# Token-tile projections 512 columns wide, one run of attention, and covered tiles that are cleared later, in a two-layer hybrid decoder on one core

## The chip, the cores and the metric

The kernel runs on one core of a Trainium2 chip. The core has a matrix engine (TensorE: PE in the profile, with its weight loads as a row of their own, PEld), a vector engine (VectorE: DVE), a scalar engine (ScalarE: ACT), GpSimd (POOL) and a queue engine that issues most transfers (SyncE: SP). Matmuls write PSUM, which this program uses as eight buffers of 128 partitions by 512 float32 values, called banks here. The metric is the device time of one execution in microseconds. The kernel before takes 1861.66 us, the median of three runs (1861.14 to 1863.24).

## The reference

Two layers work on 512 tokens of width 1024. Each layer is a half-step SwiGLU, a mixer with three head groups on one projection, and another half-step SwiGLU:

```python
for l in range(DEPTH):                                   # DEPTH = 2
    x = x + 0.5 * swiglu(rms_norm(x, ffn1_norm[l]), ffn1_w_in[l], ffn1_w_out[l])
    h = rms_norm(x, mix_norm[l]) @ w_mix_in[l]
    (c_x, c_b, c_c, h_q, h_f, h_i, h_g, f_q, f_k, f_v, f_f) = split(h)
    y = concatenate([short_conv_mixer(c_x, c_b, c_c, ...),        # 256 channels
                     hgrn2_mixer(h_q, h_f, h_i, h_g, ...),        # 4 heads of 64
                     fox_mixer(f_q, f_k, f_v, f_f, ...)], -1)     # 8 heads of 64
    x = x + y @ w_mix_out[l]
    x = x + 0.5 * swiglu(rms_norm(x, ffn2_norm[l]), ffn2_w_in[l], ffn2_w_out[l])
```

`fox_mixer` is causal softmax attention. It normalises each head's queries and keys by their root mean square and adds a cumulated decay to the logits. Its queries, keys and values are 512 columns of `w_mix_in` each, 8 heads of 64. `hgrn2_mixer` is a gated linear recurrence in chunks of 64 tokens.

## The kernel before, in words

**Precision.** Each float32 operand is held as a high and a low part of a rounded type, and each product is three matmuls: high by high (line 308), high by low (314), low by high (315). The parts of a weight come from a cast on ScalarE (297 or 766) and a subtraction on VectorE (298 or 768). The tiles of parts are called `hl`, the loaded weights `st` or `w`.

**A stream.** `stream_steps` multiplies a strip of weights by the activations, two blocks of 128 rows at a time. Such a pair of blocks is a granule: one load into `st` (two buffers), one split into `hl` (three buffers), then its matmuls. It yields after each granule. In the last granule the jobs (one per output) are done one after another; in the others all jobs take the first block, and then all the second.

**The mixer.** Three projections come first. Then two generators `hgrn`, for two pairs of HGRN heads, run in turn. After each of their steps the host loop advances another generator, `projections`, by one granule, so that dense matmuls stand between the small ones of the recurrence. `projections` calls `fox_qkv` twice, for heads 0 to 3 and 4 to 7. Each call makes queries, keys and values with `tokens`: the stationary operand is a block of 128 tokens, 256 weight columns move, and four token tiles share two banks. That is 24 granules of 24 matmuls in a layer.

After a stream `fox_qkv` normalises. For queries and keys ScalarE squares a bank into the tile `qk` (1395), VectorE sums the squares (1396), six small instructions on 128x8 values follow, and VectorE multiplies the bank by the result into `qk` (1403). That multiplication is the last reader of the bank. For values ScalarE writes the high part (1409) and VectorE the low (1410).

Then `fox_attend` runs over 16 items (4 heads, 4 query tiles), twice. An item has scores (1450 to 1452), a softmax, transposes (1513) and, every second item, products with the values (1472). `fox_prep` (transposes at 1424) makes a head ready. Beside the first half stand the 12 granules of `conv` and beside the second the 12 of `most`, which is the output projection for six of the eight row blocks. From the third item on each item gets one granule.

**The banks.** `mm` has 3, `sc` 2, `pt` 2 and `po` 1. `tokens` takes `mm`, once also `po`. The outputs of `hgrn` go to `po`.

**The feed-forward part.** `plan` writes out a fixed order of products over three chunks of the hidden width. A product is 24 matmuls of 256 columns; a unit of two feed-forward tiles has seven (P1, P2, P6, P5, P7, P3, P4). P1, P6, P7 and P4 accumulate in one bank, P5 and P3 in another, and between P6 and P7 ScalarE has to copy the first bank (872); P5's bank is copied at 875, ahead of P3. At product n the weights of product n + 3 are split (766, 768), and `run(n)` starts loads and sums for later products. The orders on ScalarE and VectorE are fixed by `follow`.

The last three of the four feed-forward parts begin with four covered tiles (0 to 3) that are multiplied in the plain way while the operands of the plan are made ready (`enter`). `clear` scales two banks of such a tile by the norm (530, 531) and applies the gate (262, tile `gi`); `values` makes the hidden value (669, 666). The dictionary `entry` says after which product of the plan that is done. Tile 2 is cleared at product 5 and tile 3 at product 8.

Of the kernel before, what the change touches and what calls it, by code (L numbers as in the profile page):

```python
# [8 lines left out]
F32 = mybir.dt.float32  # L9
F32R = mybir.dt.float32r  # L10
# [3 lines left out]
AF = mybir.ActivationFunctionType  # L14
# [142 lines left out]
class Trunk:  # L157
# [383 lines left out]
    def enter(self, fp, w_in, then):  # L541
# [73 lines left out]
        def values(f, i):  # L615
# [106 lines left out]
    def halved(self, fp, w_in, w_out, covered):  # L722
# [116 lines left out]
        for n, (kind, w, p) in enumerate(seq):  # L839
# [128 lines left out]
    def mix(self, l, w, w_out, conv_w, out_gain, q_gain, k_gain, f_bias, next_gain):  # L968
# [3 lines left out]
        with tc.tile_pool(name=self.n("mix"), bufs=1) as mp:  # L972
# [38 lines left out]
            def tokens(a, banks=("mm", "mm")):  # L1011
                bs = [self.bank(t) for t in banks]
                jobs = []
                for i in range(4):
                    acc = bs[i // 2][:, 256 * (i % 2) : 256 * (i % 2) + 256]
                    jobs.append((acc, slice(0, 256), TOK[i]) + ((False,) if i % 2 else ()))
                yield from self.stream_steps(jobs, cols((a, 256)), self.xact, KD)
                return bs

            with tc.tile_pool(name=self.n("hg"), bufs=1) as hp:  # L1020
# [52 lines left out]
                half = [{}, {}]  # L1073

                def projections():
                    for hf in range(2):
                        yield from self.fox_qkv(mp, hf, tokens, half)

                dense = projections()
# [11 lines left out]
            with tc.tile_pool(name=self.n("at"), bufs=1) as ap_:  # L1091
# [16 lines left out]
                def beside(attend, dense):  # L1108
                    for n, _ in enumerate(attend):
                        if n >= 2:  # L1110
                            next(dense, None)
                    for _ in dense:
                        pass

                self.begin_norm(next_gain)
                order = [2, 3, 4, 5, 0, 1, 6, 7]
# [22 lines left out]
                beside(self.fox_attend(ap_, 0, half[0], qkg), conv())  # L1139
                beside(self.fox_attend(ap_, 1, half[1], qkg), most())  # L1140
# [42 lines left out]
    def hgrn(self, l, pr, hp, z, q, q2, v, sg, og):  # L1183
# [142 lines left out]
        ob = self.bank("po")  # L1326
# [59 lines left out]
    def fox_qkv(self, mp, hf, tokens, half):  # L1386
        nc = self.nc
        qk = mp.tile([P, 4, 4, 2, HD], F32, tag="qk", name=self.n("qk"), bufs=2)
        for w, a in enumerate((F_Q, F_K)):
            for bi, bank in enumerate((yield from tokens(a + 256 * hf, ("mm", "po" if w and not hf else "mm")))):  # L1390
                src = bank.rearrange("p (i h d) -> p i h d", i=2, h=4)
                s8 = lambda tag: mp.tile([P, 2, 4], F32, tag=tag, name=self.n(tag), bufs=2)
                out = qk[:, 2 * bi : 2 * bi + 2, :, w, :]
                m, r, t = s8("fm"), s8("fr"), s8("ft")
                nc.scalar.activation(out, src, AF.Square)
                nc.vector.reduce_sum(m, out, axis=AX.X)
                bc = lambda c: c[:, 2 * bi : 2 * bi + 2].unsqueeze(2).to_broadcast([P, 2, 4])
                nc.vector.tensor_mul(m, m, bc(self.inv2))
                self.act(r, m, AF.Ln, bias=self.epsc)
                self.act(r, r, AF.Exp, scale=-0.5)  # L1400
                self.rsqrt(r, m, r, t)
                nc.vector.tensor_mul(r, r, bc(self.invc))
# [217 lines left out]
```

## Time and profile before

| what | value |
|---|---|
| median of 3 runs | 1861.66 us |
| profiled execution, its own time | 1859.03 us |
| its span, first to last instruction | 1857.3 us |
| granted TensorE clock | 1.000 |
| layer 0: recurrence with the attention projections beside it | 391.31 to 484.10 us |
| layer 1: the same | 1307.83 to 1400.60 us |
| PE busy in the first of these | 91.41 of 92.79 us |

The busy time of PE is from rows whose ends are modelled: matmuls are pipelined, and a row of 0.28 us is followed 0.12 us later by the next. How long a matmul holds the engine is read from the starts of successive rows; a longer distance than usual between two starts is a wait, even where no idle time is shown. In rows of instructions the columns are start, length, engine, source line, operation, output and inputs, shape and count, and in brackets the idle time before and what ended it. In grouped rows they are busy time and mean length in ns, then idle time and what ended it. Several engines write two starts closer than the length of a row, for the same reason.

### The profile page before, as it was taken

How to read it: one execution, taken by the hardware profiler on the slowest of the kernel's cores; microseconds unless marked ns; L12 is line 12 of the kernel's file. 1: busy time of each engine (PE TensorE's matmuls, PEld its weight loads, DVE VectorE, ACT ScalarE, POOL GpSimd, SP SyncE). 2: the span in 40 equal slices, each digit the busy share in tenths (PEclk: the TensorE clock that was granted, in tenths of full speed). 3: DMA queues.
4: the chain of work that ended last, by engine and by line, in shares of the span. 5: the costliest groups of instructions: out<-in, count | busy, mean ns of one | idle time of the engine just before them, and what ended most of it. 6: DMA issues, size and time to landing. Idle time of an engine off the chain costs nothing. (4 is left out here: it accounts for less than half of the span.)

```text
span 1857.3 us, 33371 instructions
## 1 busy us (share of the span) xinstructions
PE 1829.2 (98%) x13536; PEld 1699.6 (92%) x13536; DVE 1480.8 (80%) x2101; ACT 1006.4 (54%) x1467; POOL 177.3 (10%) x182
## 2 busy tenths in 40 slices
PE   8999999999999999999999999999999999999999
PEld 6899999899878899999889999998998788999997
DVE  7889787677887888879678887966868878888883
ACT  5455554564676455555445555545546664555552
POOL 0011120100000001112001111201000000020210
PEclk9999999999999999999999999999999999999999
DMA  7658783232322757868265797813323228577662
GB/s 204 170 121 191 179 179 93 74 93 69 76 79 92 216 123 171 185 169 171 80 203 120 163 193 185 170 59 90 81 64 86 80 91 227 148 156 197 147 138 91
DMA packets 245417, 251.90 MB, mean 136 GB/s; under 512 B 19568, under 2 KB 230000, under 8 KB 245264
## 3 DMA queue, kind: packets, MB, share of 16 engines
q1 hardware_dynamic: 191664, 183.69, 32.3%
q0 software_dynamic: 53600, 66.09, 22.3%
q8 instruction: 106, 1.74, 0.4%
q14 instruction: 47, 0.39, 0.1%
HBM read 223.98 MB, written 2.10 MB: 122 GB/s over the span
## 5 line engine op out<-in xcount | busy, mean ns | idle before, releaser
L766 ACT CAST hl<-w 128x1024 fp32r<-128x1024 f32 x322 | 337.1, 1049 | 324.5 <-PE mm L315 79.4
L768 DVE TENSOR_TENSOR hl<-w,hl 128x1024 fp32r<-128x1024 f32 x322 | 392.7, 1221 | 92.6 <-ACT hl L766 92.6
L298 DVE TENSOR_TENSOR hl<-st,hl 128x512 fp32r<-128x512 f32 (+2 forms) x196 | 166.5, 852 | 114.4 <-ACT hl L297 113.2
L297 ACT CAST hl<-st 128x512 fp32r<-128x512 f32 (+2 forms) x196 | 146.5, 750 | 185.0 <-PE mm L315 66.7
L308 PE MATMUL mm<-xc,hl 128*128 128x256 f32 (+1 forms) x732 | 201.6, 276 | 2.0 <-ACT g L872 1.8
L315 PE MATMUL mm<-xc,hl 128*128 128x256 f32 x728 | 201.3, 276 | 0.0
L314 PE MATMUL mm<-xc,hl 128*128 128x256 f32 x728 | 201.3, 276 | 0.0
L308 PE MATMUL sc<-xc,hl 128*128 128x256 f32 (+1 forms) x530 | 146.6, 277 | 2.9 <-ACT g L872 2.6
L315 PE MATMUL sc<-xc,hl 128*128 128x256 f32 x528 | 146.3, 277 | 0.0
L314 PE MATMUL sc<-xc,hl 128*128 128x256 f32 x528 | 146.2, 277 | 0.0
L308 PEld LDWEIGHTS mm<-xc,hl 128*128 128x128 f32 x732 | 137.3, 188 | 2.7 <-ACT g L872 2.2
L315 PEld LDWEIGHTS mm<-xc,hl 128*128 128x128 f32 x728 | 136.7, 188 | 0.1
L314 PEld LDWEIGHTS mm<-xc,hl 128*128 128x128 f32 x728 | 136.7, 188 | 0.0
L308 PE MATMUL pt<-xc,hl 128*128 128x256 f32 (+1 forms) x484 | 133.2, 277 | 2.4 <-ACT g L872 2.4
L314 PE MATMUL pt<-xc,hl 128*128 128x256 f32 x480 | 133.0, 277 | 0.0
L315 PE MATMUL pt<-xc,hl 128*128 128x256 f32 x480 | 132.7, 277 | 0.0
L308 PE MATMUL mm<-hl,x 128*128 128x256 f32 (+1 forms) x384 | 112.2, 292 | 0.7 <-DVE ft L395 0.3
L308 PE MATMUL mm<-x,hl 128*128 128x512 f32 x272 | 109.8, 404 | 0.0
L315 PE MATMUL mm<-hl,x 128*128 128x256 f32 (+1 forms) x384 | 107.4, 280 | 0.0
L314 PE MATMUL mm<-hl,x 128*128 128x256 f32 (+1 forms) x384 | 107.1, 279 | 0.0
L315 PE MATMUL mm<-x,hl 128*128 128x512 f32 x272 | 106.5, 392 | 0.0
L314 PE MATMUL mm<-x,hl 128*128 128x512 f32 x272 | 106.0, 390 | 0.0
(478 smaller groups left out, 5678.0 us busy)
## 6 DMA issues: line engine op xcount, KB each, us to landing
w<-in_ffn_w_in_dram SPq DMA_DIRECT2D x140, 512.0 KB, 5.4
w<-in_ffn_w_out_dram SPq DMA_DIRECT2D x64, 512.0 KB, 3.8
w<-in_ffn_w_out_dram POOLq DMA_DIRECT2D x56, 512.0 KB, 8.7
st<-in_w_mix_in_dram SPq DMA_DIRECT2D x88, 256.0 KB, 2.7
st<-in_ffn_w_in_dram SPq DMA_DIRECT2D x72, 256.0 KB, 3.1
w<-in_ffn_w_in_dram POOLq DMA_DIRECT2D x35, 512.0 KB, 8.4
w<-S POOLq DMA_DIRECT2D x35, 512.0 KB, 4.7
st<-in_ffn_w_out_dram SPq DMA_DIRECT2D x24, 512.0 KB, 3.5
```

Source lines behind the costliest of these rows:

```text
L297: a = nc.scalar.copy(hi, src[:, c : c + w])
L298: b = nc.vector.tensor_sub(lo, src[:, c : c + w], hi)
L308: i = nc.tensor.matmul(acc[:, c], ah, bh[:, c], start=first and c.start == 0, stop=False, skip_group_check=True,)
L314: nc.tensor.matmul(acc, ah, bl, start=False, stop=False, skip_group_check=True)
L315: i = nc.tensor.matmul(acc, al, bh, start=False, stop=last, skip_group_check=True)
L766: A(nc.scalar.copy(hi, src))
L768: return lambda: V(nc.vector.tensor_sub(lo, src, hi))
```

## The change

Three things are changed.

1. `tokens` takes all 512 columns of queries, of keys or of values at once. Each of the four token tiles has a bank of its own (`mm`, `mm`, `mm`, `po`). A granule has still two blocks and is 512 KB where it was 256 KB; a new argument `halves` makes the stream yield also in the middle of a granule. So there are 24 steps in a layer as before, of 12 matmuls of 512 columns. In `fox_qkv` ScalarE now copies each bank into `qk` and squares it into a tile `sq` (from the ring `t` of eight buffers that `hgrn` uses too); VectorE sums `sq`, the small instructions work on two token tiles at once (128x16), and the multiplication works on `qk` in place. The outputs of `hgrn` go to `pt`.
2. `fox_attend` runs once over 32 items. The 24 granules of `conv` and `most` are dealt out along it, 24 for 30 items, from the fourth item on. `most` takes the conv rows before the first attention rows.
3. In the covered feed-forward parts tiles 2 and 3 are cleared at products 9 and 12 and finished at 10 and 13, and `run(n)` stands ahead of the entries of product n.

```diff
-    def stream_steps(self, jobs, parts_of, act, nk, mid=None, pre=None, given=None):
+    def stream_steps(self, jobs, parts_of, act, nk, mid=None, pre=None, given=None, halves=False):
...
+                if halves and n == len(order) // 2:
+                    yield
...
-            5: lambda: clear(2, 0),
-            6: lambda: values(2, 0),
-            8: lambda: clear(2, 1),
-            9: lambda: values(2, 1),
+            9: lambda: clear(2, 0),
+            10: lambda: values(2, 0),
+            12: lambda: clear(2, 1),
+            13: lambda: values(2, 1),
...
+            run(n)
             if n in self.entry:
                 self.entry.pop(n)()
-            run(n)
...
-            def tokens(a, banks=("mm", "mm")):
-                bs = [self.bank(t) for t in banks]
-                jobs = []
-                for i in range(4):
-                    acc = bs[i // 2][:, 256 * (i % 2) : 256 * (i % 2) + 256]
-                    jobs.append((acc, slice(0, 256), TOK[i]) + ((False,) if i % 2 else ()))
-                yield from self.stream_steps(jobs, cols((a, 256)), self.xact, KD)
+            def tokens(a):
+                bs = [self.bank(t) for t in ("mm", "mm", "mm", "po")]
+                jobs = [(b, slice(0, T), c) for b, c in zip(bs, TOK)]
+                yield from self.stream_steps(jobs, cols((a, T)), self.xact, KD, halves=True)
                 return bs
...
-                order = [2, 3, 4, 5, 0, 1, 6, 7]
+                order = [2, 3, 0, 1, 4, 5, 6, 7]
...
-                beside(self.fox_attend(ap_, 0, half[0], qkg), conv())
-                beside(self.fox_attend(ap_, 1, half[1], qkg), most())
+                dense, dealt = beside(), 0
+                for n, _ in enumerate(self.fox_attend(ap_, qkv, qkg)):
+                    while dealt < 24 * (n - 1) // 30:
+                        next(dense, None)
+                        dealt += 1
+                for _ in dense:
+                    pass
...
-        ob = self.bank("po")
+        ob = self.bank("pt")
...
+            for i, bank in enumerate(banks):
+                nc.scalar.copy(qk[:, i, :, w, :], heads(bank))
+                sq = hp.tile([P, T], F32, tag="t", name=self.n("sq"), bufs=self.tb)
+                nc.scalar.activation(sq, bank, AF.Square)
+                nc.vector.reduce_sum(m[:, i, :], heads(sq), axis=AX.X)
+            for b in range(2):
+                c = slice(2 * b, 2 * b + 2)
...
+                for i in (2 * b, 2 * b + 1):
+                    out = qk[:, i, :, w, :]
+                    nc.vector.tensor_mul(out, out, r[:, i, :].unsqueeze(2).to_broadcast([P, NH, HD]))
+        for i, bank in enumerate((yield from tokens(F_V))):
+            sc = self.invc[:, i : i + 1]
+            nc.scalar.activation(V[:, i, :, 0, :], heads(bank), AF.Copy, scale=sc)
+            nc.vector.scalar_tensor_tensor(
+                out=V[:, i, :, 1, :], in0=heads(bank), scalar=sc, in1=V[:, i, :, 0, :],
+                op0=ALU.mult, op1=ALU.subtract,
+            )
...
-        heads = range(4 * hf, 4 * hf + 4)
+        heads = range(NH)
```

The source lines of the changed kernel are up to four less or two more than those of the kernel before.

The order of instructions moves at three places. The first is ScalarE in the feed-forward part after the mixer of layer 0, from the copy of P1 of the second unit (tiles 6 and 7, products 7 to 13) to the copy of P5. The tiles `hl` are weight splits for later products, `g` with a bank as input is P1's or P6's copy, `gi` is a covered tile's gate. Before:

```order
L865 ACTIVATE g_1096_7375<-pt_7348 128x512
L766 CAST hl_7407<-w_7141 128x1024
L262 ACTIVATE g_1096_7375<-g_1096_7375 128x512
L262 ACTIVATE gi_7412<-gi_7412 128x512
L766 CAST hl_7443<-w_7179 128x1024
L872 ACTIVATE g_1104_7445<-pt_7348 128x512
L766 CAST hl_7475<-w_7212 128x1024
L875 ACTIVATE u_1107_7477<-sc_7450 128x512
```

Of the change (lines 766, 865, 872 and 875 are now 768, 867, 874 and 877):

```order
L867 ACTIVATE g_1058_6976<-pt_6949 128x512
L768 CAST hl_7008<-w_6741 128x1024
L262 ACTIVATE g_1058_6976<-g_1058_6976 128x512
L768 CAST hl_7039<-w_6782 128x1024
L874 ACTIVATE g_1064_7041<-pt_6949 128x512
L262 ACTIVATE gi_7044<-gi_7044 128x512
L768 CAST hl_7074<-w_6818 128x1024
L877 ACTIVATE u_1069_7076<-sc_7049 128x512
```

The gate of the covered tile stood two places ahead of the copy of P6's bank and now stands behind it, ahead of the copy of P5's bank.

The second place is ScalarE in layer 0 where the queries are taken out of their banks. Before, the first half of the queries:

```order
L1395 ACTIVATE qk_4156<-mm_4157 128x8x64
L297 CAST hl_4464<-st_4462 128x512
L1395 ACTIVATE qk_4156<-mm_4158 128x8x64
L262 ACTIVATE fr_4351<-fm_4350,epsc 128x8
L262 ACTIVATE fr_4351<-fr_4351 128x8
L262 ACTIVATE ft_4352<-fr_4351 128x8
```

Of the change, all the queries (`fr` and `ft` are the small tiles of the norm, `fm` the sums that VectorE makes of `sq`):

```order
L1393 COPY qk_4156<-mm_4158 128x8x64
L1395 ACTIVATE sq_4408<-mm_4158 128x512
L1393 COPY qk_4156<-mm_4159 128x8x64
L1395 ACTIVATE sq_4412<-mm_4159 128x512
L1393 COPY qk_4156<-mm_4160 128x8x64
L1395 ACTIVATE sq_4416<-mm_4160 128x512
L262 ACTIVATE fr_4405<-fm_4404,epsc 128x16
L262 ACTIVATE fr_4405<-fr_4405 128x16
L297 CAST hl_4555<-st_4553 128x1024
L1393 COPY qk_4156<-po_4161 128x8x64
L1395 ACTIVATE sq_4420<-po_4161 128x512
```

Two instructions per bank now end its use, four banks follow one another, and ahead of the fourth stand two small ones that wait for VectorE's sums and a weight split.

The third place is PE at the same moment, of the change: the last matmul of the queries, the recurrence's scores (1313, `t` are its factors) and the first matmuls of the keys.

```order
L315 MATMUL po_4161<-hl_4350,x_397_3683 128x512
L1313 MATMUL sc_4398<-t_4396,t_4392 128x2x64 x4
L308 MATMUL mm_4443<-hl_4449,x_373_3544 128x512
L314 MATMUL mm_4443<-hl_4449,x_373_3544 128x512
L315 MATMUL mm_4443<-hl_4449,x_373_3544 128x512
L308 MATMUL mm_4444<-hl_4449,x_373_3544 128x512
```

The keys follow the queries with only one step of the recurrence between, and they take the same four banks; before, the next stream took a bank that was free and one of the stream ahead of it.

More of the change, by code (lines that the diff above doesn't have):

```diff
@@ L1072, in mix @@
                 run = [self.hgrn(l, pr, hp, z[pr], q[pr], q2[pr], v, sg[pr], og) for pr in range(2)]
[L1073 to L1079, printed above, removed]
+                qkv = {}
+                dense = self.fox_qkv(mp, hp, tokens, qkv)
                 step = 0
@@ L1137, in most, with beside @@
                             add(2 * dg + i, banks[i])
[L1139 to L1140 removed]
+                def beside():
+                    yield from conv()
+                    yield from most()
+                dense, dealt = beside(), 0
[5 more added lines that the diff above has]
+                    pass
                 self.ntog = 0
@@ new lines, in fox_qkv @@
+            banks = yield from tokens(a)
+            s8 = lambda tag: mp.tile([P, 4, NH], F32, tag=tag, name=self.n(tag), bufs=2)
+            m, r, t = s8("fm"), s8("fr"), s8("ft")
+            for i, bank in enumerate(banks):
[3 more added lines that the diff above has]
+                nc.vector.reduce_sum(m[:, i, :], heads(sq), axis=AX.X)
```

52 lines of the change are left out of this document (15 added, 37 removed).

## The prediction

> **What bounds the kernel now.** I read the page's busy times first, then a window for each mixer, then the starts of matmuls.
>
> ```profile
> PE 1829.2 (98%) x13536; PEld 1699.6 (92%) x13536; DVE 1480.8 (80%) x2101; ACT 1006.4 (54%) x1467; POOL 177.3 (10%) x182
> 391.31:484.10 92.79, 91.41 (x835) 88.06 (x834) 70.74 (x158) 48.51 (x105) 1.86 (x4) 1.00 0.26 69
> 1307.83:1400.60 92.77, 91.39 (x834) 88.04 (x833) 70.69 (x158) 48.46 (x105) 1.86 (x4) 1.00 0.26 69
> ```
>
> The second and third rows are the stretch of recurrence and attention projections in each layer: length, busy time of PE, PEld, DVE, ACT and POOL, granted clock, DMA share. PE bounds everything at full clock, and the two layers agree within 0.02 us, so a saving in one counts twice. Since PE is never idle for long, only two things can help: fewer PE cycles, or the removal of small waits. Whether 512 columns are cheaper than twice 256 is read from starts:
>
> ```profile
> 370.17 0.39 PE L308 MATMUL mm<-x,hl 128*128 128x512 f32 x1
> 379.01 0.39 PE L308 MATMUL mm<-x,hl 128*128 128x512 f32 x1
> ...
> 391.86 0.28 PE L314 MATMUL mm<-hl,x 128*128 128x256 f32 x1
> ...
> 394.45 0.28 PE L315 MATMUL mm<-hl,x 128*128 128x256 f32 x1
> ...
> 1828.77 0.39 PE L308 MATMUL mm<-hl,hh 128*128 128x512 f32 x1
> 1833.53 0.39 PE L308 MATMUL mm<-hl,hh 128*128 128x512 f32 x1
> ```
>
> From 370.17 to 379.01 stand 39 matmuls of 512 columns: 8.84 / 39 = 226.7 ns. From 391.86 to 394.45 stand 22 of the attention projections' 256-column ones: 2.59 / 22 = 117.7 ns, against 226.7 / 2 = 113.3. The last two rows are 512 columns of `hl` moving over held activations, the changed form: 21 in 4.76 us, again 226.7.
>
> **Part 1, the width.** A layer has 24 granules x 24 = 576 matmuls of 256 columns, afterwards 288 of 512. At 117.7 and 226.7 ns that is 67.8 against 65.3 us: at most 2.5 us. Some of the 576 run at 113, so zero is the other end. I take 1.5 a layer, since the block quoted is a typical one.
>
> The Trainium skill, "TensorE: Matmul & The Clock Gate", section "Back-to-back issue gap", gives sustained spacings of 81 ns at 128 columns and 131 at 512. By it a pair at 256 would cost 162 ns or more against 131, an estimated 18 us or more for 576 pairs. The trace differs, with 226.7 ns at 512.
>
> The waits inside that stretch in layer 0:
>
> ```profile
> 420.23 0.28 PE L314 MATMUL mm<-hl,x 128*128 128x256 f32 x1
> 420.80 1.13 PE L1317 MATMUL sc<-t,t 128*128 128x128 f32 x8 [0.29 <-DVE fm L1398]
> ...
> 425.20 0.28 PE L315 MATMUL mm<-hl,x 128*128 128x256 f32 x1
> 425.87 1.13 PE L1317 MATMUL sc<-t,t 128*128 128x128 f32 x8 [0.39 <-DVE t L1308]
> ...
> 454.69 0.28 PE L315 MATMUL mm<-hl,x 128*128 128x256 f32 x1
> 455.13 0.36 PE L308 MATMUL mm<-hl,x 128*128 128x256 f32 x1 [0.17 <-DVE ft L395]
> ...
> 473.84 0.28 PE L315 MATMUL mm<-hl,x 128*128 128x256 f32 x1
> 474.29 0.36 PE L308 MATMUL mm<-hl,x 128*128 128x256 f32 x1 [0.17 <-DVE qk L1403]
> ```
>
> The distances less 0.12 are 0.45, 0.55, 0.32 and 0.33 us: 1.65. The first two are scores behind a VectorE that is busy with normalising, the last two a stream that waits for a bank which only the normalising multiplication releases. What the change does to the two engines, by these rows:
>
> ```profile
> L298 DVE TENSOR_TENSOR hl<-st,hl 128x512 fp32r<-128x512 f32 x128 | 87.9, 688 | 60.2 <-ACT hl L297 59.7
> L297 ACT CAST hl<-st 128x512 fp32r<-128x512 f32 x128 | 78.7, 617 | 97.5 <-PE mm L315 58.0 <-PE po L315 25.7 <-issue 6.5
> L298 DVE TENSOR_TENSOR hl<-st,hl 128x1024 fp32r<-128x1024 f32 x60 | 73.2, 1222 | 53.8 <-ACT hl L297 53.2
> L297 ACT CAST hl<-st 128x1024 fp32r<-128x1024 f32 x60 | 62.9, 1048 | 84.7 <-PE pt L315 29.2 <-PE po L315 25.7 <-DMA st<-in_ffn_w_out_dram 8.7
> L1396 DVE TENSOR_REDUCE fm<-qk 128x8 f32<-128x512 f32 x8 | 5.5, 682 | 3.5 <-ACT qk L1395 3.5
> L1403 DVE TENSOR_TENSOR qk<-mm,fr 128x512 f32<-128x512 f32 x7 | 4.8, 687 | 0.1
> L1395 ACT ACTIVATE qk<-mm 128x512 f32<-128x512 f32 x7 | 4.1, 591 | 2.4 <-PE mm L315 2.4
> L262 ACT ACTIVATE fr<-fm,epsc 128x8 f32<-128x8 f32 x8 | 2.4, 298 | 4.9 <-DVE fm L1398 4.9
> L395 DVE SCALAR_TENSOR_TENSOR ft<-fm,ft 128x8 f32<-128x8 f32 x8 | 1.3, 166 | 1.1 <-ACT ft L262 1.1
> ```
>
> Per layer: 24 splits become 12 of double size, ScalarE 24 x 0.617 = 14.8 to 12 x 1.048 = 12.6, VectorE 16.5 to 14.7. Eight sums and eight multiplications remain. The small instructions halve: 20 fewer on VectorE at about 0.16, 3.2 us, and 12 fewer on ScalarE at 0.2 to 0.3, about 3. ScalarE gains 8 copies of about 0.59: 4.7. VectorE thus loses some 5 us of 70.7, ScalarE stays level. None of it is on PE's path; it only moves when operands and banks come. A bank is now free after two ScalarE instructions, 1.2 us, without the way over VectorE, but all four are wanted at once by the next stream.
>
> At the queries' end (order above) I count from their last matmul. Two banks are then some 3.6 us old (twelve matmuls of the other two, 2.7, and a recurrence step of about 0.9, less than the 1.13 of its rows above, whose end overlaps the next matmul), so ScalarE is through with them. It is through with the third near 0; two norm instructions follow (0.5, and perhaps 0.6 until VectorE has the sums), then a split of 1.05, and the fourth bank is copied and squared by about 3.3. PE does the scores (0.9) and nine matmuls (2.0) first and wants the fourth bank at 2.9: a wait of about 0.4. At the keys' end no norm instruction stands ahead: none. VectorE's burst (four sums, four multiplications, 5.5 us, in place of two and two) falls into the next recurrence steps, for which the new order puts 26 matmuls, 5.9 us, ahead of the next scores; I leave 0.5 for it. So of 1.65 us of waits 0.9 comes back: 0.75 is gained, and with the width 2.25 a layer, **4.5 us**. Bounds: all waits gone, 4.15 a layer; and the loss of rival A.
>
> The load queue has 12 loads of 512 KB for 24 of 256 KB, the same bytes at a DMA share of 0.26, and every step has the PE time of before: nothing. The eight `sq` tiles in the ring of eight take places whose readers are done two steps earlier; if that cover fails, each costs one sum, 0.68. The recurrence's outputs in `pt` meet two buffers where one served; nothing, at worst 1.2 us a layer for the two ScalarE reads that free it.
>
> **Part 2, one run of attention.** At the joint of the halves:
>
> ```profile
> 534.91 0.48 PE L308 MATMUL mm<-hy,hl 128*128 128x512 f32 x1
> 535.23 0.40 PE L314 MATMUL mm<-hy,hl 128*128 128x512 f32 x1
> 535.72 0.39 PE L1472 MATMUL po<-PH,V 128*128 128x256 f32 x1
> ...
> 542.95 0.22 PE L1450 MATMUL sc<-KA,QA 128*128 128x128 f32 x1
> 543.47 0.30 PE L1451 MATMUL sc<-KB,QB 66*128 66x128 f32 x1 [0.31 <-issue]
> ```
>
> Here 0.49 stands for 0.227 and 0.52 for some 0.15, about 0.6 us of waits, and the mixed order there pays about 0.09 for changes between kinds of matmul (0.32 for 0.227 at 534.91), perhaps five more than elsewhere. I take 1.0 a layer, **2.0 us**. The dense work is the same 24 granules of 12 matmuls (2.7 us), 24 in 29 items where it was 12 in 12 twice; the items without any (first and last two of each half) become fewer. The third granule of `most` needs heads 0 to 3, ready at item 16, and stands at item 20: four items of cover. Bounds: nothing, and 3 us a layer if the spread helps elsewhere.
>
> **Part 3, clearing later.** The same wait stands in all three covered parts:
>
> ```profile
> 679.48 0.28 PE L315 MATMUL sc<-xc,hl 128*128 128x256 f32 x1
> 680.95 0.39 PE L308 MATMUL pt<-xc,hl 128*128 128x256 f32 x1 [1.19 <-ACT g L872]
> ...
> 1010.40 0.39 PE L308 MATMUL po<-xc,hl 128*128 128x256 f32 x1 [1.70 <-ACT g L872]
> ...
> 1597.51 0.39 PE L308 MATMUL pt<-xc,hl 128*128 128x256 f32 x1 [1.19 <-ACT g L872]
> ...
> 676.78 0.63 ACT L262 ACTIVATE g<-g 128x512 f32<-128x512 f32 x1
> 678.83 0.63 ACT L262 ACTIVATE gi<-gi 128x512 f32<-128x512 f32 x1 [1.42 <-DVE gi L530]
> 679.37 1.03 ACT L766 CAST hl<-w 128x1024 fp32r<-128x1024 f32 x1
> 680.31 0.59 ACT L872 ACTIVATE g<-pt 128x512 f32<-128x512 f32 x1
> ```
>
> P7 waits for the copy of P6, which stands on ScalarE behind the gate of tile 3, which waits 1.42 for VectorE. Without that gate the split starts at 677.4, the copy is done by 679.0, and P7 can start at 679.6. The three waits shown are 1.19 + 1.70 + 1.19 = 4.1 us. The gate of tile 2 now stands ahead of the copy of P5, which P3 needs at 682.3, a product of 2.7 us later; the gate waits for VectorE until about 680.1, ends at 680.7, a split ends at 681.7 and the copy at 682.3: just in time. I take **4.0 us**; if it comes late by 0.5 each, 2.6.
>
> **Sum.** 4.5 + 2.0 + 4.0 = 10.5 us, a span of 1846.8 after 1857.3. The profiled execution is 2.6 us below the median of the runs shown; the difference carried over to the median of 1861.7 gives **1851.2 us**.
>
> **The rivals.**
> A, slower: the four banks. At queries to keys and keys to values, in both layers, ScalarE finishes late: eight reads x 0.59 = 4.7, a split 1.05 and two norm instructions 0.5 make 6.3 us if it starts only at the last matmul, and PE wants the fourth bank at 2.9: 3.4 each, 13.6 in all. With part 1's 4.5 lost too: 1861.7 - 6.0 + 13.6 = 1869. It is slower than before from 1.5 us a change of streams without part 1's gain. For it: ScalarE is in order, and its norm instructions have waited 4.9 us for VectorE. Against: 48.5 of 92.8 us busy, and two banks are done early.
> B, the stretch gains nothing, since VectorE's burst makes waits as long as those removed: 1861.7 - 6.0 = 1855.7. For it: DVE is busy 70.7 of 92.8 and it ended the waits above.
> C, all bounds on the good side: 8.3 + 6 + 4.1, 1843. For it: nearly every wait listed ends on something that is moved.
> D, weight loads set the pace, at PEld's 92% busy: 576 fewer loads by 0.188 us, or 108 us, 1753. The groups' loads are that long:
>
> ```profile
> L308 PEld LDWEIGHTS mm<-hl,x 128*128 128x128 f32 x176 | 33.2, 188 | 1.3 <-issue 1.2
> ```
>
> Against it: matmuls start 117.7 ns apart, closer than 188, so loads overlap too.
>
> **How the numbers follow.** Forecast 0.52, A 0.17, B 0.17, C 0.11, D 0.01, and 0.02 for no effect. A measurement here tells about 0.2%, 3.7 us, from no change. Faster: forecast, C, D and 0.12 of B, 0.76; the same: 0.05 of B, 0.02, and a mild A, 0.03: 0.10; slower: the rest of A, 0.14. The forecast's own range is 1846 to 1855; B and C and a mild A lie in 1839 to 1862, the range.
>
> **What would show it.** Spacing of 512-column `hl,x` matmuls near 227 ns; the rows of the stretch near 90.5 us; no wait on the P6 copy in the second unit of the three covered parts, and none at P3. I am wrong on part 1 if PE stands over 1 us at the first matmul on the fourth bank of the keys or values, or if the scores wait over 0.5 us several times; on part 2 if the attention has new waits on VectorE in its later heads.

## The result, and the profile after

The changed kernel takes 1860.11 us, the median of 14 executions, against 1861.38 us for the kernel before, also of 14; 1851.2 us was forecast. The ratio is 0.9996 with a 95% interval of 0.9986 to 1.0005: no difference that can be told. What changed is the spread. The 14 executions of the kernel before lie between 1859.94 and 1863.89 us, those of the changed kernel between 1852.91 and 1867.39 us.

The profiled execution is the shortest of the 14, with a span of 1851.1 us after 1857.3. So the profile shows a gain of 6.2 us that most executions do not have, and that its 1852.91 us lies near the forecast is the luck of which execution was profiled. First the busy times, from the page of the changed kernel:

```profile
PE 1828.0 (99%) x12960; PEld 1672.2 (90%) x12960; DVE 1472.3 (80%) x2029; ACT 1006.8 (54%) x1427; POOL 177.0 (10%) x182
```

TensorE has 576 matmuls less, as the width says, and is still never idle for long. The next rows are windows of both kernels, of layer 0: the attention projections, from the start of their first to that of their last matmul, and the whole mixer, from the first matmul of the value stream of the recurrence to the first of the next feed-forward part. The columns are length, busy time of PE, PEld, DVE, ACT and POOL, granted clock, DMA share and GB/s. Before:

```profile
391.66:483.98 92.32, 90.94 (x831) 87.59 (x829) 70.27 (x156) 48.04 (x104) 1.86 (x4) 1.00 0.26 70
379.69:602.41 222.72, 219.68 (x1570) 193.72 (x1568) 176.43 (x380) 134.11 (x290) 6.19 (x12) 1.00 0.30 83
```

After:

```profile
392.25:483.79 91.54, 90.37 (x543) 73.52 (x541) 67.42 (x123) 48.45 (x89) 2.38 (x6) 1.00 0.23 68
380.28:602.29 222.01, 219.41 (x1282) 180.04 (x1280) 173.15 (x345) 134.73 (x271) 5.97 (x12) 1.00 0.29 83
```

The stretch lost 0.78 us and the mixer 0.71, where 2.25 and 3.25 were forecast. The rest of the gain in the profile is in the three covered feed-forward parts. There the second unit no longer waits for the copy of P6; the timeline of TensorE at the start of its P7, after (where the kernel before had 1.19 us at 680.95):

```profile
678.94 0.28 PE L315 MATMUL sc<-xc,hl 128*128 128x256 f32 x1
679.06 0.28 PE L308 MATMUL pt<-xc,hl 128*128 128x256 f32 x1
679.18 0.28 PE L314 MATMUL pt<-xc,hl 128*128 128x256 f32 x1
```

The starts are 0.12 us apart, so nothing is waited for. But a new wait has come at P2 of the third unit, product 15, in the second and the third covered part (the columns are start and length, then the instruction):

```profile
1017.33 0.28 PE L315 MATMUL mm<-xc,hl 128*128 128x256 f32 x1
1017.55 0.36 PE L308 MATMUL po<-xc,hl 128*128 128x256 f32 x1
1017.75 0.28 PE L314 MATMUL po<-xc,hl 128*128 128x256 f32 x1
```

Instead of 0.113 the distances are 0.22 and 0.20: 0.2 us lost. VectorE tells why. Before:

```profile
1018.59 0.69 DVE L669 TENSOR_TENSOR hq<-g,u 128x512 f32<-128x512 f32 x1
1019.19 0.68 DVE L666 SCALAR_TENSOR_TENSOR hq<-g,po 128x512 f32<-128x512 f32 x1
1020.02 1.23 DVE L768 TENSOR_TENSOR hl<-S,hl 128x1024 fp32r<-128x1024 f32 x1 [0.15 <-ACT hl L766]
```

After:

```profile
1014.93 0.68 DVE L532 TENSOR_TENSOR gi<-pt,inv 128x512 f32<-128x512 f32 x1
1015.53 0.68 DVE L533 TENSOR_TENSOR ui<-pt,inv 128x512 f32<-128x512 f32 x1
1016.13 0.68 DVE L671 TENSOR_TENSOR hq<-g,u 128x512 f32<-128x512 f32 x1
1016.73 0.68 DVE L668 SCALAR_TENSOR_TENSOR hq<-g,po 128x512 f32<-128x512 f32 x1
```

The two products of P4 (669 and 666 before, 671 and 668 now) are the last to read the bank `po`, which P2 writes next. The clear of tile 3, moved from product 8 to 12, now stands ahead of them and costs 1.2 us, so they end at 1017.4. A wait of 0.2 us looks like nothing. It turned out to matter for more than its length.

### The profile page after: what moved, and what is told of

The parts are those of the page before. It is cut to its first block, busy times and chain, and to the rows that moved or that the text cites. A ratio compares the mean times of both kernels' runs of the same rounds, so it can differ in the third digit from the quotient of the medians.

```text
span 1851.1 us, 32009 instructions
## 1 busy us (share of the span) xinstructions
PE 1828.0 (99%) x12960; PEld 1672.2 (90%) x12960; DVE 1472.3 (80%) x2029; ACT 1006.8 (54%) x1427; POOL 177.0 (10%) x182
## 4 chain that ended last, share of the span: by engine, by line
PE 88%; DVE 6%; ACT 3%; issue 2%; DMA 1%; SPq 0%; ACTq 0%
PE mm L308 12%; PE mm L314 12%; PE mm L315 12%; PE sc L308 6%; PE sc L315 6%; PE sc L314 6%; PE pt L308 6%; PE pt L314 6%; PE pt L315 6%; PE po L308 3%; PE po L314 3%; PE po L315 3%; DVE hl L298 1%; PE po L1472 1%; PE sc L1313 1%
## 5 line engine op out<-in xcount | busy, mean ns | idle before, releaser
L298 DVE TENSOR_TENSOR hl<-st,hl 128x1024 fp32r<-128x1024 f32 (+2 forms) x172 | 162.8, 949 | 124.4 <-ACT hl L297 123.9
L297 ACT CAST hl<-st 128x1024 fp32r<-128x1024 f32 (+2 forms) x172 | 142.1, 828 | 163.5 <-PE po L315 67.9
L308 PEld LDWEIGHTS sc<-xc,hl 128*128 128x128 f32 x530 | 99.5, 188 | 3.3 <-ACT g L874 2.1
L314 PEld LDWEIGHTS sc<-xc,hl 128*128 128x128 f32 x528 | 99.3, 188 | 0.0
L315 PEld LDWEIGHTS sc<-xc,hl 128*128 128x128 f32 x528 | 99.1, 188 | 0.1
```

What stands on the lines that cost most here:

```text
L297: a = nc.scalar.copy(hi, src[:, c : c + w])
L298: b = nc.vector.tensor_sub(lo, src[:, c : c + w], hi)
L308: i = nc.tensor.matmul(acc[:, c], ah, bh[:, c], start=first and c.start == 0, stop=False, skip_group_check=True,)
L314: nc.tensor.matmul(acc, ah, bl, start=False, stop=False, skip_group_check=True)
L315: i = nc.tensor.matmul(acc, al, bh, start=False, stop=last, skip_group_check=True)
```

## The experiments

All the kernels compute the whole reference. "Before" in a comparison is the kernel before in the same session, with medians from 1861.37 to 1862.10 us.

**Which part spreads the times.** Four kernels: part 3 alone; the changed kernel without part 3; part 1 alone; part 2 alone.

```diff
# e1: the kernel before with
-            5: lambda: clear(2, 0),
+            9: lambda: clear(2, 0),      # and products at 10, 12, 13; run(n) ahead of the entry
# e2: the changed kernel with that undone
# e3: e2, and the attention in two halves with the old order of granules
# e4: the kernel before with
+                for n, _ in enumerate(self.fox_attend(ap_, half, qkg)):   # 32 items, 24 granules dealt out
```

> The kernel before with part 3 alone (clears and products two later entries, next unit's early work run before the entry). Theory S (part 3 does all that the profile shows, and the spread of the changed kernel, 1853 to 1867 us, comes from part 1 or 2): the waits on the copy of P6 in the second unit are gone, median 1855 to 1858 (4 to 6 us less than before), spread of the runs 4 us or less like the kernel before. Theory C (part 3 itself makes the spread, because the pool's accumulating transfers or the weights of the clear come late in some runs): spread over 8 us, median 1859 to 1862.

> The changed kernel with part 3 undone (parts 1 and 2 alone). Theory S: the sum of excess over nominal spacing in the mixers is 1 to 2 us less than before, but the runs spread over 8 us or more and the median is 1861 to 1865, no better than before. Theory C: spread 4 us or less, median 1860 to 1862.

> The kernel before with part 1 alone (512 columns over four banks, attention in two halves as before). Theory W (the 512 KB loads into two staging buffers land late in some runs): spread over 8 us and median 1861 to 1866. If part 1 is not the cause of the spread: 4 us or less, median 1860 to 1862 (0.3 to 1.5 us gained, as the profile of the changed kernel shows for this stretch). The forecast of the record would be 1857.2.

> The kernel before with part 2 alone (one run of attention over eight heads, dense granules dealt along it, 256 columns kept). Forecast of the record: 1859.7. Theory W: spread 4 us or less, median 1860 to 1862. Theory R (the run of attention makes the spread): spread over 8 us, median over 1861.

| kernel | median, us | lowest to highest | ratio to before, 95% |
|---|---|---|---|
| part 3 alone | 1862.55 | 1856.03 to 1867.22 | 1.0004 (0.9995 to 1.0014) |
| parts 1 and 2 | 1860.26 | 1859.07 to 1862.34 | 0.9996 (0.9987 to 1.0004) |
| part 1 alone | 1860.24 | 1859.06 to 1862.12 | 0.9994 (0.9986 to 1.0003) |
| part 2 alone | 1863.63 | 1862.03 to 1866.91 | 1.0015 (1.0006 to 1.0023) |

The spread belongs to part 3, as theory C has it, and theories S, W and R fall. The reason that theory C gives, transfers or weights that come late in some runs, is not what the later traces show. Windows of the mixers give the sizes of the other two; for part 1 alone, then both parts, then part 2 alone, layers 0 and 1:

```profile
380.56:602.82 222.26, 219.44 (x1281) 179.73 (x1280) 173.14 (x344) 134.05 (x270) 5.97 (x12) 1.00 0.30 83
1296.64:1518.98 222.34, 219.61 (x1281) 179.70 (x1280) 173.14 (x344) 134.05 (x270) 5.97 (x12) 1.00 0.30 83
```

```profile
381.75:603.90 222.15, 219.52 (x1281) 180.03 (x1280) 173.13 (x345) 134.82 (x271) 5.97 (x12) 1.00 0.30 83
1298.19:1520.48 222.29, 219.53 (x1281) 180.09 (x1280) 173.14 (x345) 134.76 (x271) 5.97 (x12) 1.00 0.30 83
```

```profile
381.53:605.89 224.36, 220.23 (x1569) 194.24 (x1568) 176.51 (x381) 134.90 (x291) 5.97 (x12) 1.00 0.31 82
1300.63:1523.70 223.07, 220.14 (x1570) 194.16 (x1568) 176.52 (x381) 134.89 (x291) 5.97 (x12) 1.00 0.31 82
```

Against 222.72 and 222.74 before, part 1 gains 0.46 and 0.40 us, part 2 adds 0.11 and 0.05 to that, and alone it loses 1.64 and 0.33. These are differences of single executions. In layer 0 the mixer takes 222.72 to 223.46 us in the nine profiles whose mixer is that of the kernel before (median 222.85), 222.01 to 222.91 in the eight with parts 1 and 2 (median 222.22), and 222.26 and 222.18 in the two with part 1 alone. So part 1 gains some 0.6 us there, and no gain of part 2 can be told.

**Which half of part 3.** The later entries alone, and the early work ahead of the entry alone. The second half moves one instruction on one engine: VectorE's total S3 of the first unit goes ahead of the first products. Two more profiles of the spreading kernels were taken with them.

```diff
# e5: later entries only            # e6: only this
-            if n in self.entry:
-                self.entry.pop(n)()
             run(n)
+            if n in self.entry:
+                self.entry.pop(n)()
# e7: the changed kernel again; e8: e1 again
```

> Half of part 3 alone: the kernel before with the clears and products at items 9, 10, 12 and 13, each entry still ahead of the item's own early work for later units. Theory L (the later place of the clear makes the spread of part 3, 1856 to 1867 us): spread over 8 us, median 1861 to 1864. Theory E (the early work run ahead of the entry makes it): spread 4 us or less and median 1856 to 1859.

> The other half of part 3 alone: the kernel before with each item's early work run ahead of the entry, clears at 5, 6, 8 and 9 as before. Theory L: spread 4 us or less, median 1860 to 1863 (the waits on the copy of P6, 4.1 us in all, stay). Theory E: spread over 8 us, median 1860 to 1864.

> The changed kernel again, for a profile of another of its executions (1853 to 1867 us). If it is a longer one, the added time stands in the three covered parts (around 640 to 720, 960 to 1040 and 1560 to 1620 us) by theory L or E, as one to three new waits of TensorE of 2 to 5 us each, on a weight split whose total or load came late; by a theory of general noise it is spread over the whole span.

> The kernel with part 3 alone again, for the same reason: if longer than 1860 us, its excess over the profiled 1856.03 us stands in the covered parts by theory L or E, and elsewhere or everywhere by noise.

The later entries alone gave 1857.56 us (1855.90 to 1858.02), ratio 0.9977 (0.9968 to 0.9987); the early work alone 1860.28 us (1858.79 to 1861.78), ratio 0.9993 (0.9984 to 1.0002). Both were narrow, so neither half seemed to make the spread. The two further profiles were of short executions again, 1855.23 and 1857.13 us, so no added time could be located in them. I took it that the two halves only spread together (theory I below).

**Together or not, and in which covered part.** The changed kernel without the early work; part 1 with the later entries; and the later entries with the early work in one covered part only.

```diff
# e9: the changed kernel, run(n) behind the entry again
# e10: e3 with the later entries
# e11, e12: e5, and in the first, or the third, of the three covered parts
+            if early:
+                run(n)
             if n in self.entry:
```

> The changed kernel with one thing undone: each item's early work stands again behind the entry, so on VectorE the total S3 of the first unit follows the first products. Theory I (the spread comes only where the early total and the late clear meet; alone each gains): the gains add, 1860.26 with parts 1 and 2 less the 4.2 us of the late entries, median 1855.5 to 1856.5, spread 4 us or less. Theory N (the late clear spreads in company of parts 1 and 2 whatever stands first): spread over 8 us, median 1858 or more.

> Part 1 (512 columns) and the late entries, attention in two halves, early work behind the entry. Theory I with a part 2 that gains nothing: median 1855.5 to 1856.5, spread 4 us or less, level with the run before this one within 0.5 us. If part 2 gains 2.0 us as forecast, this kernel is 2 us slower than that one.

> The late entries in all three covered parts, the early work ahead of the entry only in the first of the three. Theory P (each covered part adds its share of the spread, 0 to 4 us): lowest near 1856, median 1858 to 1860, spread 4 to 7 us. If this part alone makes it: median 1861 to 1863, spread over 8 us. If it has no share: median 1857 to 1858, spread 3 us.

> The same with the early work ahead of the entry only in the third of the covered parts. Theory P: lowest near 1856, median 1858 to 1860, spread 4 to 7 us; alone the cause: 1861 to 1863 and over 8 us; no share: 1857 to 1858 and 3 us.

| kernel | median, us | lowest to highest | ratio to before, 95% |
|---|---|---|---|
| e9 | 1859.62 | 1855.33 to 1866.08 | 0.9989 (0.9980 to 0.9998) |
| e10 | 1859.20 | 1855.27 to 1865.10 | 0.9982 (0.9973 to 0.9992) |
| e11 | 1860.99 | 1856.62 to 1865.61 | 0.9997 (0.9986 to 1.0007) |
| e12 | 1858.33 | 1856.27 to 1862.38 | 0.9986 (0.9978 to 0.9995) |

Theory I falls: e9 and e10 have no early work and spread all the same. So e11 and e12 cannot be read as the share of one part (theory P), though e12's numbers would fit. But now a profile had caught a long execution, e10 with 1865.10 us. Its windows behind P2 of the third unit, in the second and the third covered part:

```profile
1021.00:1137.00 116.00, 116.00 (x987) 116.00 (x986) 95.10 (x98) 60.10 (x68) 14.39 (x12) 1.00 0.74 171
1610.50:1726.50 116.00, 116.00 (x987) 116.00 (x986) 95.18 (x98) 60.10 (x68) 14.37 (x12) 1.00 0.74 171
```

and the same work in the profiled execution of the changed kernel:

```profile
1018.00:1129.00 111.00, 111.00 (x982) 111.00 (x981) 93.97 (x98) 59.89 (x68) 14.37 (x12) 1.00 0.76 178
1602.40:1713.40 111.00, 111.00 (x982) 111.00 (x981) 93.97 (x98) 59.79 (x68) 14.34 (x12) 1.00 0.76 179
```

TensorE is never idle in either, at the same clock. But 116.00 / 987 is 117.5 ns and 111.00 / 982 is 113.0 ns a matmul. Counted from start to start, every matmul of 256 columns in e10's stretch holds the engine for 117.8 ns, and for 113.3 in the other, which makes 4.4 us over the 984 of a stretch. Three such stretches, one in each covered part, would make 13 us, near the 14.5 us between the shortest and the longest execution of the changed kernel. This execution of e10 has two of them, 8.7 us, and lies 9.8 us above the shortest of its nine.

I then read the spacing from all profiles so far, 12 runs and the two kernels. A stretch keeps one of the two spacings until TensorE waits, and has one of the two after the wait: of 221 waits over 70 ns in the feed-forward parts 63 were followed by the long one (in most of the first 20 matmuls behind the wait). Nine of the profiles have the later entries, 27 stretches behind P2. The wait of 0.2 us stands in 7, where the 190 matmuls ahead of it ran at the short spacing and so came 0.8 us earlier; 4 of these 7 stretches are long. In the other 20 there is no wait, and all are short. The first product of each chunk begins with a matmul in two pieces of 128 columns (the argument `parted` of `mm3`), and behind all 168 such places the spacing is short. In the kernel before nothing waits between there and the end of the stretch. The profile of e5 has the 190 matmuls at the long spacing in all three parts, so that no wait came. That this held in all its executions is a guess. And e5 to e8 ran in one session, on a chip on which no other experiment ran: there all nine such stretches (e5, e7, e8) are long, in the other profiles 11 of 18. So the narrow times of e5 may belong to the session and not to the kernel; neither e1 nor the changed kernel was run there more than once. If a long stretch came in 4 of 27 cases everywhere, ten executions without any would have an estimated chance below 1 in 100 (23/27 to the power 30). So the draws are not alike everywhere, and what they depend on stays open.

**Is it the spacing.** The changed kernel with pieces behind the new wait; with the clear one product later, so that the wait goes; with pieces at every product; and the kernel before without any.

```diff
# e13
-                kind == "I" and p == "P1" and w in (covered, *(f0 for f0, _ in CHUNKS)),
+                kind == "I" and p in ("P1", "P2") and w in (covered, *(f0 for f0, _ in CHUNKS)),
# e14
-            12: lambda: clear(2, 1),
-            13: lambda: values(2, 1),
+            13: lambda: clear(2, 1),
+            14: lambda: values(2, 1),
# e15: True in that place; e16: the kernel before with False
```

> The changed kernel, with the first matmul of P2 in each first unit of a chunk also in two pieces of 128 columns, as P1 has it (57 + 113 + 170 ns in the trace, the same 340 as three whole ones). Theory T (a stretch keeps one of two paces, 113.3 or 117.8 ns, drawn at each restart after a wait, and pieces always bring the fast one): the wait of 0.2 us at P2 may stay, the stretches behind it (1018 to 1135 and 1602 to 1715 us) run at 113.3 in every execution, median 1854 to 1857, spread 5 us or less. If the pace is not the cause of the spread: median 1859 to 1861, spread over 8 us.

> The changed kernel, with the second late clear at item 13 and its products at 14, so that VectorE's two products that free the bank for P2 stand ahead of the clear. Theory T: no wait at P2 of the third unit, hence no new draw, pace 113.3 there, median 1854 to 1857, spread 5 us or less. Otherwise: 1859 to 1861, spread over 8 us.

> The changed kernel, with the first matmul of every product of the weight-reuse part in two pieces. Theory T: all stretches there run at 113.3 (in the profiles 191 matmuls behind the wait at P5 and 211 of the last chunk are often slow, 0.85 and 0.93 us each, up to three and four times), median 1852 to 1856, spread 4 us or less. If each piece costs more than the 340 ns allow: slower than 1860.

> The kernel before without any pieces. Theory T: after each wait the pace is drawn for the whole stretch to the next wait, some 250 us (2,000 matmuls of 256 columns, 9 us) three times, more for the first unit: lowest near 1860, highest 1875 or more, median 1864 to 1875, spread over 10 us. If pieces do nothing: 1861, spread 4 us.

| kernel | median, us | lowest to highest | ratio to before, 95% |
|---|---|---|---|
| e13, pieces at P2 | 1857.13 | 1855.31 to 1858.07 | 0.9971 (0.9961 to 0.9981) |
| e14, clear after P4 | 1865.29 | 1857.03 to 1871.55 | 1.0017 (1.0005 to 1.0030) |
| e15, pieces everywhere | 1892.67 | 1892.36 to 1893.36 | 1.0164 (1.0151 to 1.0177) |
| e16, before, no pieces | 1867.90 | 1859.91 to 1884.42 | 1.0033 (1.0013 to 1.0052) |

With pieces behind the wait the spread is 2.8 us in eight executions, as theory T has it, and the median lies 0.1 us above its range. The changed kernel itself was not run again beside these four; e14 and e16, on the same chip, do spread. Taking the pieces out of the kernel before makes a spread of 25 us where its own executions, taken beside these four, lie within 2.8. The profile of that kernel, 1884.42 us, has the long spacing over 1,918 matmuls in a row in each of the three covered parts. At 4.4 ns each that is 25 us, and its shortest execution lies 24.5 us lower. Two of its windows in the second and third covered part:

```profile
1060.00:1100.00 40.00, 40.00 (x342) 40.00 (x341) 33.75 (x35) 20.88 (x24) 9.82 (x8) 1.00 0.90 173
1650.00:1690.00 40.00, 40.00 (x342) 40.00 (x341) 34.58 (x37) 20.57 (x24) 9.57 (x8) 1.00 0.86 161
```

(342 matmuls in 40 us; 356 and 355 in the same windows of the kernel before.)

Two expectations missed by more. In e14 the wait at P2 is gone. But the tile's products, now at product 14, stand on VectorE ahead of the subtraction (870) that P2's gate needs, and behind that gate ScalarE splits the first hidden operand, `m`. TensorE waits for its low part. VectorE, then TensorE, in the second covered part:

```profile
1024.48 0.42 DVE L671 TENSOR_TENSOR hq<-gi,ui 128x256 f32<-128x256 f32 x1
1024.82 0.42 DVE L668 SCALAR_TENSOR_TENSOR hq<-gi,ui 128x256 f32<-128x256 f32 x1
1025.15 0.68 DVE L870 TENSOR_TENSOR g<-g,po 128x512 f32<-128x512 f32 x1
...
1027.48 1.23 DVE L722 TENSOR_TENSOR m<-hq,m 128x1024 fp32r<-128x1024 f32 x1 [0.51 <-ACT m L722]
```

```profile
1028.47 0.28 PE L308 MATMUL sc<-m,hl 128*128 128x256 f32 x1
1028.76 0.38 PE L314 MATMUL sc<-m,hl 128*128 128x256 f32 x1
```

The start of 1028.76 is 0.17 us late, the next one 0.11, and the spacing is drawn anew four products behind the pieces, for the rest of the stretch. In this profiled execution, 1857.03 us, it came out short in all three parts; the others reach 1871.55. A still shorter wait stands two products earlier, at the start of P6:

```profile
1022.66 0.28 PE L315 MATMUL po<-xc,hl 128*128 128x256 f32 x1
1022.78 0.33 PE L308 MATMUL mm<-xc,hl 128*128 128x256 f32 x1
1022.94 0.28 PE L314 MATMUL mm<-xc,hl 128*128 128x256 f32 x1
```

The distance of 0.16 is 0.05 us too long. The matmuls ahead of it stand 113.3 ns apart, the 47 behind it, up to the wait at 1028.76, 117.8; in the third covered part the same delay was followed by the short spacing. So this miss fits the theory, and a wait of 0.05 us is enough for a change. In e15 I had counted the pieces as free. They are not: a pair of pieces is one matmul more, with its own distance.

```profile
PE 1869.5 (99%) x13305; PEld 1713.4 (91%) x13305; DVE 1474.5 (78%) x2029; ACT 1010.9 (53%) x1427; POOL 177.0 (9%) x182
```

13305 less 12960 are 345 matmuls, and the spans differ by 1890.6 - 1851.1 = 39.5 us: 0.114 us each. One pair repays that only ahead of a long stretch.

**What the parts are worth then.** Three pieces, at P2 of the third unit in the covered parts, with part 3 alone and with the whole change.

```diff
+                    or p == "P2" and w == CHUNKS[1][0] and covered < FIRST
```

> The kernel before with part 3, and pieces at P2 of the third unit in the three covered parts only (three more matmuls, 0.11 us each by the runs with pieces everywhere). Theory T: part 3 then keeps its gain in every execution: 1861.6 less 4.6 us of waits and 0.7 at the first unit, plus 0.6 for the new waits and 0.3 for the pieces: 1857.6, spread 5 us or less. By the share of the draw without pieces (1862.6 was measured) it would be 1860 or more with a spread over 8 us.

> The changed kernel with the same three pieces. Theory T: 1857.1 as measured with twelve pieces, less nine of 0.11 us: 1856.1, spread 5 us or less; 1.1 to 1.5 us less than the run before this one, which is what the 512 columns gave alone, with nothing for the one run of attention. If that run of attention gains its 2.0 us once the pace is settled, 3 us less.

Part 3 alone with the pieces takes 1856.12 us (1854.42 to 1861.24), ratio 0.9974 (0.9964 to 0.9985); the whole change with them 1853.46 us (1852.78 to 1857.82, five executions), ratio 0.9956 (0.9944 to 0.9968). Both gained more than expected. The interval of the last lies below that of the changed kernel, 0.9986 to 1.0005. The spreads, 6.8 and 5.0 us, are wider than e13's: three of ten and one of five executions are still 4 to 5 us longer than the next shorter one, about one stretch. Which one was not seen, since both profiles are of shorter executions. So three pieces do not hold the spacing in every execution.

The 2.7 us between the two medians lie near the 3 us that were expected if part 2 gains its 2.0. Their profiles do not bear that out. The mixer of layer 0, with part 3 alone and with the whole change:

```profile
382.22:605.14 222.92, 219.79 (x1570) 194.25 (x1569) 176.34 (x380) 134.09 (x290) 6.19 (x12) 1.00 0.31 83
380.51:602.84 222.33, 219.54 (x1282) 180.16 (x1280) 173.21 (x345) 134.69 (x271) 5.97 (x12) 1.00 0.30 83
```

The mixers differ by 0.59 us here and by 0.47 in layer 1, no more than part 1 gives. Of the 3.4 us between the two spans, 1.7 lie ahead of this mixer (382.22 against 380.51), where the kernels are the same.

## Why the prediction was wrong, by its own steps

**What bounds the kernel.** That only cycles of TensorE and its small waits count, held. But the rows 117.7 and 113.3 ns, which stood in the prediction, were read as the price of a width and an ideal. They are two spacings of the same matmul, and the time after a wait depends on which one follows it. That is where the sum of 10.5 us went wrong: it priced a wait by its length alone, and 1860.11 us were measured where it gave 1851.2.

**Part 3, forecast 4.0 us.** The mechanism was right. The three waits are gone, by distances of starts 1.36 + 1.86 + 1.36 = 4.6 us, nothing new stands at P3, and the earlier total brings 0.2 us more in each part (the waits at the first unit go from 1.46 and 0.33 to 1.03 and 0.52). The later entries alone were worth 4.2 us (e5), and part 3 with pieces 6.0. The step that failed is the search for what is late next. The prediction followed the moved gate on ScalarE, to the copies of P5 and P6, and stopped; the moved multiplications stand on VectorE ahead of P4's products, which free the bank of P2. They cost 0.2 us there and a new draw of the spacing, up to 4.4 us, in as many as three places. Without pieces the gain was gone in the median: 1862.55 us for part 3 alone.

**Part 1, forecast 4.5 us.** Measured 0.86 in the two mixers and 1.1 in the median. The width was mis-sized: in the stretch before, some 270 of 576 matmuls had the long spacing, which is 270 x 4.4 ns = 1.2 us to win at most, where 2.5 was the bound and 1.5 the price; and with 512 columns some 70 of 288 are still 4 ns or more over. VectorE was to lose 5 us in the stretch and lost 2.9 (70.27 to 67.42). The net of waits failed too. The list of four waits, 1.65 us, left out a fifth of 0.52 us in the kernel before, also at the scores behind VectorE:

```profile
429.08 0.28 PE L314 MATMUL mm<-hl,x 128*128 128x256 f32 x1
429.71 1.13 PE L1317 MATMUL sc<-t,t 128*128 128x128 f32 x8 [0.36 <-DVE t L1308]
```

So there were some 2.2 us of waits, not 1.65, and they became 1.66, not 0.9. VectorE's burst, for which 0.5 us was left, makes two waits of 0.60 and 0.51 us per layer at the scores; VectorE and TensorE in the changed kernel:

```profile
425.85 1.29 DVE L1407 TENSOR_TENSOR qk<-qk,fr 128x512 f32<-128x512 f32 x2
427.06 0.17 DVE L397 SCALAR_TENSOR_TENSOR ft<-fm,ft 128x16 f32<-128x16 f32 x1
427.15 0.69 DVE L1304 TENSOR_TENSOR t<-t,q 128x512 f32<-128x512 f32 x1
```

```profile
427.98 1.13 PE L1313 MATMUL sc<-t,t 128*128 128x128 f32 x8 [0.44 <-DVE ft L398]
433.10 0.57 PE L1313 MATMUL sc<-t,t 128*128 128x128 f32 x3 [0.35 <-DVE t L1304]
```

The scores' operand `t` stands behind the normalising multiplications, and the 26 matmuls of cover were not enough. A third wait, 0.55 us, came at the first attention stream, whose third bank is one that the value stream of the recurrence still holds:

```profile
394.26 0.50 PE L308 MATMUL mm<-hl,x 128*128 128x512 f32 x1 [0.38 <-DVE zf L1067]
```

So rival B was right that VectorE's burst makes new waits, and right on their size if one takes the prediction's own four, 1.65 us; with the fifth, 0.55 us a layer was gained. The gain in the stretch, 0.78 us in these two profiles, is still less than the waits and the width give together; the rest went into the recurrence's own matmuls, whose steps of 128 columns take 0.7 us longer and were not looked into. Rival A was wrong: in neither layer does a wait over 0.14 us stand at the fourth bank. The 0.4 us that the forecast itself had there did not come either.

**Part 2, forecast 2.0 us.** Measured 0.16 in the two mixers with part 1, less than profiles of the same mixer differ, and a loss of 2.0 without it. The waits at the joint are gone (0.26, 0.21 and 0.47 us, from 535.23 to 542.95), but in the same place of the changed kernel's layer 0 stand 0.48, 0.23, 0.49 and 0.45, two of them behind VectorE's `KB` and ScalarE's `PH`. So the step that failed is the price of the joint: its waits were exchanged for others. Alone, 1.18 us of its loss in layer 0 are one wait at the last products with the values, where 0.47 stood before; ScalarE, then TensorE, in that profile:

```profile
593.56 1.05 ACT L297 CAST hl<-st 128x1024 fp32r<-128x1024 f32 x1 [3.39 <-DMA st<-in_ffn_w_in_dram]
595.14 0.38 PE L1473 MATMUL po<-PH,V 128*128 128x256 f32 x1 [1.01 <-ACT PH L1516]
```

The cast `PH` stands behind a weight split whose load came late. In layer 1 this wait is absent, and the rest of the loss was not followed up.

**The sum.** The rows priced at 10.5 us were worth 1.3 in the median as the change stands, which cannot be told from nothing, and 8.6 (1862.10 - 1853.46) with three pieces. That the second number is nearer the forecast does not confirm its terms: parts 1 and 2 are worth some 1.3 us in the mixers, not 6.5, and in the covered parts 374 matmuls of the kernel before ran at the long spacing in its profile, 1.6 us, and none in that of the whole change with pieces.

## What to carry to other kernels

Where an engine is full, a wait costs its length and what it does to the work behind it: compare the spacing of equal instructions before and after it, in more than one execution. If a change widens the spread, treat that as its own result and profile until a long execution is caught; one profile of the shortest execution says little of the median. And when a step moves, follow it on every engine on which it has instructions, to the buffers that the work behind it frees.

## What the hardware showed that was not expected

Matmuls of the same form, at a granted clock of 1.00, run at 113.3 or 117.8 ns from start to start, and keep one of the two for up to 1,918 in a row (e16, at 117.8). In these traces they change only where TensorE waits, once for no more than 0.05 us (e14), or at a matmul in two pieces, which was followed by the short spacing in 168 of 168 places. What draws the spacing at a wait stays open.

The Trainium skill, "TensorE: Matmul & The Clock Gate", section "Part 1: The HAM clock gate", says that TensorE falls to half its clock after an idle window of some 3.4 us. No wait here is that long, so no run shows it: the waits in these stretches are 0.05 to 1.9 us, the clock in the windows is 1.00, and the difference is 4%.

To issue one matmul in two pieces costs 0.114 us more, as much as a whole matmul of 256 columns, although the two have no more columns than the one: in the profile their starts are 57 ns apart, the next matmul starts 113 ns behind the second, and the one after it 170 ns on.
